# Strided attention on one core: instruction streams moved to a 128-instruction border near their beginning, and constants made by merged operations

## The chip, the cores and the metric

The kernel runs on one core of a Trainium2 chip. A core has five engines with an instruction stream each: TensorE (PE in the profile, with PEld for its weight loads), VectorE (DVE), ScalarE (ACT), GpSimd (POOL) and SyncE (SP), which here only issues transfers. Sixteen DMA engines move the data between HBM and the on-chip memory SBUF. The metric is the time of one execution on the device, in microseconds (us).

## The reference: what is computed

Attention in which every one of the 1024 query positions attends to the same 16 keys, those at the positions 0, 64, 128, ... The inputs Q, K, V are float32 of shape (8, 12, 1024, 64); only the 16 rows of K and V that are attended are ever read.

```python
attend_positions = np.arange(0, seq, stride)          # stride 64: 16 keys
q = Q[:, :, i:i + 1, :]
k = K[:, :, attend_positions, :]
v = V[:, :, attend_positions, :]
scores = np.einsum('bhqd,bhkd->bhqk', q, k) * scale   # scale = 1/sqrt(64)
weights = np.exp(scores - np.max(scores, axis=-1, keepdims=True))
weights = weights / (np.sum(weights, axis=-1, keepdims=True) + 1e-10)
result[:, :, i, :] = np.einsum('bhqk,bhkd->bhqd', weights, v)[:, :, 0, :]
```

## The kernel before

The 96 pairs of batch and head are worked in 24 groups (NG) of four heads (HG). One group is 1 MB of Q and 1 MB of output, so about 50 MB pass through the DMA engines; K and V are 384 KB each.

All transfers are issued by SP, in program order, on one queue. First comes K (`k_raw`, L98), then group 0 of Q (`load(0)`, through the helper `_copy` at L35), then V (`v_raw`, L100), then the Q groups 1 to 9: there are ten buffers for Q (QBUFS) and eight for the output (OBUFS). After that each turn of the main loop issues `store(g)` and then `load(g + 10)`. The first two Q loads are cut into 128 pieces, the later ones into 32.

The head of the kernel builds constants while the first transfers are under way:
- GpSimd makes an identity matrix (`make_identity`, two operations in masks.py), two index tiles (`iota_p`, `col4`, L112 and L114), and by eight copies (L118) the permutation `perm_v`, which spreads the 16 rows of V over 128 partitions; then it clears the larger part of `k_t` (L129).
- VectorE clears the first part of `k_t` (L123) and three weight buffers (L127), works out from the partition number to which of four heads a partition belongs (`slot_i` L132, `slot_f` L137, `s_sel` L139), copies this selector into the last four columns of three value buffers (L145), and makes `mask` from it (L148).
- ScalarE casts K (`key_rows`, L158), VectorE transposes it (`k_r`, L159), and both place it in `k_t` (`keys`, L169).

Then each group goes through the same stations: `cast` to bf16, half by GpSimd (L200) and half by ScalarE (L201); `transpose` on VectorE (L205); `scores`, four matmuls (L212) and the exponential on ScalarE (L223); `values`, the masked V of the group, on GpSimd (L191); `outputs`, eight matmuls (L237) and then reciprocal (L245) and product (L247) on VectorE, with the last part copied by ScalarE (L249) and scaled by GpSimd (L250). Each value buffer carries the selector beside the values, so that the matmul also yields the sum of the weights. The order on each engine is the order of the program (`manual_schedule`); `ahead(g)` puts the casts, transposes and scores of the next groups between the outputs of group g.

Nothing in the program says where an engine's instructions lie in memory. Each engine's stream is fetched in pieces while the kernel runs.

Of the kernel before, what the change touches and what calls it, by code (L numbers as in the profile page):

```python
# [9 lines left out]


FP32 = mybir.dt.float32
BF16 = mybir.dt.bfloat16
I16 = mybir.dt.int16
I32 = mybir.dt.int32
AF = mybir.ActivationFunctionType
ALU = mybir.AluOpType


def _ap_with(ap: bass.AP, new_ap, extra_offset: int = 0) -> bass.AP:  # L20
    return dataclasses.replace(
        ap, ap=[list(p) for p in new_ap], offset=ap.offset + extra_offset
    )


def _copy(nc, out: bass.AP, in_: bass.AP):

    sides = [
        mybir.BassSymbolicTensorAccessPattern(
            ap=side.ap, dtype=side.dtype, bass_ap=side,  # L30
            is_dma=True, for_custom_bir_dma=True,
        )
        for side in (in_, out)
    ]
    return nc.sync.add_instruction(  # L35
        mybir.InstDMACopy(
            name=nc.get_next_instruction_name(), engine=mybir.EngineType.SP,
            ins=sides[:1], outs=sides[1:], queue="qSPDynamicHW",
            mode="Copy",
        )  # L40
    )
# [9 lines left out]
def kernel(  # L51
# [8 lines left out]
    nc = tc.nc  # L60

    B, H, S, D = Q.shape
    NK = S // stride
    scale = 1.0 / math.sqrt(D)

    P = 128
    HG = 4
    NG = B * H // HG
    NC = NG // 2
    SD = S * D  # L70
    KW = P + NK
# [4 lines left out]
    const = ctx.enter_context(tc.tile_pool(name="const", bufs=1))  # L76
# [7 lines left out]

    ctx.enter_context(tc.manual_schedule())


    k_raw = const.tile([P, NC, D], FP32, name="k_raw")
    v_raw = const.tile([P, NC, D], FP32, name="v_raw")
# [3 lines left out]
    def load(g):  # L93
        qn[g] = qn_pool.tile([P, 32 * D], FP32, name="qn", tag="qn")
        n = P if g < 2 else 32
        _copy(nc, qn[g], _ap_with(Q, [[HG * SD // n, n], [1, HG * SD // n]], g * HG * SD))

    nc.sync.dma_start(k_raw, _ap_with(K, kv_src))  # L98
    load(0)
    nc.sync.dma_start(v_raw, _ap_with(V, kv_src))  # L100
    for g in range(1, QBUFS):
        load(g)


    identity = const.tile([P, P], BF16, name="identity")
    make_identity(nc, identity)
    id_v = identity.rearrange("p (c b a k) -> p c b a k", c=2, b=2, a=2)

    perm_v = const.tile([P, 2, 2, 2, 2, NK], BF16, name="perm_v")

    iota_p = const.tile([P, 1], I16, name="iota_p")
    nc.gpsimd.iota(iota_p, pattern=[[0, 1]], base=0, channel_multiplier=1)  # L112
    col4 = const.tile([P, 4], I16, name="col4")
    nc.gpsimd.iota(col4, pattern=[[1, 4]], base=0, channel_multiplier=0)  # L114
    for c in range(2):
        for a in range(2):
            for e in range(2):
                nc.gpsimd.tensor_copy(  # L118
                    out=perm_v[:, c, a, :, e], in_=id_v[:, c, :, a]
                )  # L120

    k_t = const.tile([P, NG, 2, KW], BF16, name="k_t")
    nc.vector.memset(k_t[:, 0:8], 0.0)  # L123
    w_bufs = []
    for i in range(3):
        w = const.tile([P, 8, P], BF16, name=f"w{i}")
        nc.vector.memset(w, 0.0)  # L127
        w_bufs.append(w)
    nc.gpsimd.memset(k_t[:, 8:NG], 0.0)  # L129

    slot_i = const.tile([P, 1], I16, name="slot_i")
    nc.vector.tensor_scalar(  # L132
        out=slot_i, in0=iota_p, scalar1=4, scalar2=3,
        op0=ALU.logical_shift_right, op1=ALU.bitwise_and,
    )
    slot_f = const.tile([P, 1], FP32, name="slot_f")
    nc.vector.tensor_copy(out=slot_f, in_=slot_i)  # L137
    s_sel = const.tile([P, 4], BF16, name="s_sel")
    nc.vector.tensor_scalar(  # L139
        out=s_sel, in0=col4, scalar1=slot_f, scalar2=None, op0=ALU.is_equal  # L140
    )
    v_bufs = []
    for i in range(3):
        v = const.tile([P, 4 * D + 4], BF16, name=f"v{i}")
        nc.vector.tensor_copy(out=v[:, 4 * D :], in_=s_sel)  # L145
        v_bufs.append(v)
    mask = const.tile([P, 4, D], BF16, name="mask")
    nc.vector.tensor_copy(out=mask, in_=s_sel.unsqueeze(2).to_broadcast([P, 4, D]))  # L148

    k_bf = const.tile([P, NC, D], BF16, name="k_bf")  # L150
# [182 lines left out]
```

## Time and profile before

| what | value |
|---|---|
| median of 3 runs | 129.21 us (129.13 to 129.32) |
| span of the profiled execution, first to last instruction | 127.7 us |
| the runs' median beyond this span | 1.5 us |
| PE, DVE, ACT, POOL busy | 50%, 69%, 67%, 63% of the span |
| data moved | 25.95 MB read, 25.17 MB written |
| DMA engines busy with data | 96.7% of the span |
| instruction packets within the span | 5 on queue q14, 2 on queue q8 |

The page gives no other time of the profiled execution than its span. A row of the groups of instructions reads: line, engine, operation, output from input, shapes, count, busy time and the mean of one. A row of the timeline begins with start and duration in us. A row of the table by stages has the stretch, its length, the busy time (and count) of PE, PEld, DVE, ACT and POOL, the granted clock of TensorE, the mean share of the sixteen DMA engines, and GB/s. There a packet is counted whole in the stretch in which it starts, so the share of a short stretch can be above 1. In the rows of queues, the last number is the time of the packets as a share of sixteen engines over the stretch asked for. In the rows of transfers, it is the time from issue to landing.

### The profile page before, as it was taken

How to read it: one execution, taken by the hardware profiler on the slowest of the kernel's cores; microseconds unless marked ns; L12 is line 12 of the kernel's file. 1: busy time of each engine (PE TensorE's matmuls, PEld its weight loads, DVE VectorE, ACT ScalarE, POOL GpSimd, SP SyncE). 2: the span in 40 equal slices, each digit the busy share in tenths (PEclk: the TensorE clock that was granted, in tenths of full speed). 3: DMA queues.
4: the chain of work that ended last, by engine and by line, in shares of the span. 5: the costliest groups of instructions: out<-in, count | busy, mean ns of one | idle time of the engine just before them, and what ended most of it. 6: DMA issues, size and time to landing. Idle time of an engine off the chain costs nothing.

```text
span 127.7 us, 1234 instructions
## 1 busy us (share of the span) xinstructions
PE 63.5 (50%) x292; PEld 29.8 (23%) x292; DVE 88.5 (69%) x167; ACT 86.1 (67%) x120; POOL 80.1 (63%) x89
## 2 busy tenths in 40 slices
PE   0006559256756628653696646366777646410000
PEld 0002223123322313332243313133423313200000
DVE  6956691869698696859769799797987976720000
ACT  4161917886999968999958979979787885320000
POOL 8933709554875876577866997969689694450000
PEclk9999999996799986999559999999856999955555
DMA  2999989998997998989989999999999999999980
GB/s 66 379 320 467 472 349 482 380 452 354 467 482 326 498 413 369 495 362 421 493 357 431 470 380 444 434 403 462 428 393 449 398 428 418 428 426 421 431 352 36
DMA packets 7911, 51.20 MB, mean 401 GB/s; under 512 B 3872, under 2 KB 3872, under 8 KB 3872
## 3 DMA queue, kind: packets, MB, share of 16 engines
q1 hardware_dynamic: 7904, 51.12, 96.7%
q8 instruction: 2, 0.03, 0.1%
q14 instruction: 5, 0.04, 0.1%
HBM read 25.95 MB, written 25.17 MB: 400 GB/s over the span
## 4 chain that ended last, share of the span: by engine, by line
POOL 37%; issue 33%; DVE 10%; PE 6%; ACT 2%; POOLq 1%; DVEq 0%
POOL qb L200 15%; POOL out_sb L250 12%; POOL v L191 10%; PE sc L212 4%; DVE out_sb L247 3%; PE o_ps L237 2%; DVE s_sel L139 2%; POOLq L328 1%; DVE w L127 1%; DVE qt L205 1%; ACT qb L201 1%; DVE rec L245 1%; DVE k_t L123 1%; ACT out_sb L249 1%; ACT k_t L169 0%
## 5 line engine op out<-in xcount | busy, mean ns | idle before, releaser
L237 PE MATMUL o_ps<-v,w 128*128 128x260 bf16 x192 | 37.9, 316 | 37.3 <-DVE out_sb L247 33.2
L250 POOL TENSOR_TENSOR out_sb<-out_sb,rec 128x768 f32<-128x768 f32 x24 | 35.3, 1472 | 29.2 <-ACT out_sb L249 29.2
L247 DVE TENSOR_TENSOR out_sb<-o_ps,rec 128x768 f32<-128x768 f32 (+1 forms) x48 | 39.6, 825 | 1.6
L223 ACT ACTIVATE w<-sc 64x512 bf16<-64x512 f32 x48 | 35.3, 736 | 5.0 <-PE sc L212 4.6
L205 DVE STREAM_TRANSPOSE qt<-qb 128x1024 int32<-128x1024 int32 x24 | 29.5, 1230 | 11.1 <-ACT qb L201 7.1
L212 PE MATMUL sc<-qt,k_t 128*128 128x512 bf16 x96 | 31.7, 463 | 10.4 <-DVE qt L205 10.4
L237 PEld LDWEIGHTS <-w 128*128 128x128 bf16 x192 | 18.6, 108 | 60.5 <-DVE out_sb L247 41.6
L249 ACT COPY out_sb<-o_ps 128x768 f32<-128x768 f32 x24 | 19.2, 800 | 15.8 <-DVE rec L245 15.5
L200 POOL CAST qb<-qn 128x1024 bf16<-128x1024 f32 x24 | 25.0, 1040 | 4.1 <-DMA qn<-in_Q_dram 4.1
L201 ACT CAST qb<-qn 128x1024 bf16<-128x1024 f32 x24 | 25.0, 1047 | 0.7
L245 DVE RECIPROCAL rec<-o_ps 128x12 f32<-128x12 f32 (+1 forms) x72 | 15.1, 210 | 5.6 <-PE o_ps L237 5.2
L191 POOL TENSOR_TENSOR v<-mask,v_rep 128x256 bf16<-128x256 bf16 x24 | 16.1, 670 | 1.0 <-DVE v_rep L184 1.0
L212 PEld LDWEIGHTS <-k_t 128*128 128x128 bf16 x96 | 10.7, 111 | 21.1 <-ACT k_t L169 8.0
L169 ACT COPY k_t<-k_r 32x128 bf16<-32x128 bf16 x20 | 5.9, 296 | 2.3 <-DVE k_r L159 2.0
L129 POOL MEMSET k_t<- 128x4608 bf16 x1 | 3.9, 3937 | 0.0
L184 DVE CAST v_rep<-vp 128x384 bf16<-128x384 f32 x4 | 2.2, 542 | 1.9 <-PE vp L180 1.8
L158 ACT CAST k_bf<-k_raw 128x256 bf16<-128x256 f32 x3 | 1.2, 408 | 2.9 <-DMA k_raw<-in_K_dram 2.9
L139 DVE TENSOR_SCALAR s_sel<-col,slot_f 128x4 bf16<-128x4 int16 x1 | 2.6, 2553 | 0.1
L159 DVE STREAM_TRANSPOSE k_r<-k_bf 128x128 int32<-128x128 int32 x3 | 0.9, 309 | 2.3 <-ACT k_bf L158 2.3
L180 PE MATMUL vp<-v_bf,perm_v 128*128 128x384 bf16 x4 | 1.6, 412 | 1.1 <-DVE v_rep L184 0.6
L158 ACT ACT_TABLE_LOAD x1 | 1.3, 1283 | 0.7 <-PEq L314 0.7
L123 DVE MEMSET k_t<- 128x1152 uint32 x1 | 1.0, 1018 | 1.0 <-PEq L314 1.0
(17 smaller groups left out, 6.6 us busy)
## 6 DMA issues: line engine op xcount, KB each, us to landing
qn<-in_Q_dram SPq DMA_DIRECT2D x24, 1024.0 KB, 16.0
out_dram<-out_sb SPq DMA_DIRECT2D x24, 1024.0 KB, 14.8
k_raw<-in_K_dram SPq DMA_DIRECT2D x1, 384.0 KB, 4.2
v_raw<-in_V_dram SPq DMA_DIRECT2D x1, 384.0 KB, 7.2
```

What stands on the lines that cost most here:

```text
L169: op(k_t[dst : dst + 32, 8 * m + c : 8 * m + 8 : 2, :, col : col + NK], k_r[src : src + 32, 4 * m : 4 * m + 4].rearrange("p n (a k f) -> p ...
L191: nc.gpsimd.tensor_tensor(out=vb[g][:, 0 : 4 * D].rearrange("p (s d) -> p s d", s=4), in0=mask, in1=v_rep[:, g // 2, g % 2].unsqueeze(1).t ...
L200: nc.gpsimd.tensor_copy(out=qb[g][:, 0:half], in_=qn[g][:, 0:half])
L201: nc.scalar.copy(qb[g][:, half:], qn[g][:, half:])
L205: nc.vector.transpose(qt[g].bitcast(I32), qb[g].bitcast(I32))
L212: nc.tensor.matmul(sc, lhsT=k_t[:, g, f, NK * (1 - e) : NK * (1 - e) + P], rhs=_ap_with(q, [q.ap[0], [D, 8], [16 * D, 2], [2, 32]], extra_ ...
L223: nc.scalar.activation(out=_ap_with(wa, [wa.ap[0], [P, 8], [1, 2], [2, 32]], extra_offset=64 * a), in_=sc[64 * a : 64 * a + 64].rearrange( ...
L237: nc.tensor.matmul(ps[:, i, 0 : 4 * D + 4], lhsT=wt[g][:, i0 + i], rhs=vb[g], start=True, stop=True,)
L245: nc.vector.reciprocal(r, ps[:, 0:n, 4 * D : 4 * D + 4])
L247: nc.vector.tensor_tensor(out=to, in0=o, in1=by, op=ALU.mult)
L249: nc.scalar.copy(to, o)
L250: nc.gpsimd.tensor_tensor(out=to, in0=to, in1=by, op=ALU.mult)
```

## The change

Three things change, all in the head.

1. VectorE, GpSimd and SP each get one directive `addr_align(128, max_nops=0)`. The instruction that follows it is placed at the next address that is a multiple of 128 instructions, and the engine gets there by a jump over the padding rather than by running through it. VectorE's and GpSimd's stand before all their work in the kernel's body. SP's stands between the first Q load and V's load.
2. The selector is made from one index tile. `ahead4` holds 64 - 16 s + p for partition p and slot s; its bits 4 and 5 are zero where the partition belongs to the slot. Two operations with a constant operand replace the shift, the cast and the comparison with a per-partition operand. The three weight buffers and the three value buffers become slices of one tile each, so that one clear replaces three and one copy replaces three.
3. `perm_v` is made by four copies of 64 elements per partition, which read each column twice, instead of eight copies of 32.

```diff
+    for engine in (nc.vector, nc.gpsimd):
+        engine.addr_align(128, max_nops=0)
...
     nc.sync.dma_start(k_raw, _ap_with(K, kv_src))
     load(0)
+    nc.sync.addr_align(128, max_nops=0)
     nc.sync.dma_start(v_raw, _ap_with(V, kv_src))
...
-    make_identity(nc, identity)
+    w_all = const.tile([P, 3, 8, P], BF16, name="w_all")
+    v_all = const.tile([P, 3, 4 * D + 4], BF16, name="v_all")
+    w_bufs, v_bufs = [w_all[:, i] for i in range(3)], [v_all[:, i] for i in range(3)]
+
+    nc.gpsimd.iota(ahead4, pattern=[[-16, 4]], base=64, channel_multiplier=1)
+    nc.gpsimd.memset(identity, 0.0)
+    nc.gpsimd.affine_select(
+        out=identity, in_=identity, compare_op=ALU.not_equal, fill=1.0, base=0,
+        pattern=[[-1, P]], channel_multiplier=1,
+    )
...
-    nc.gpsimd.iota(iota_p, pattern=[[0, 1]], base=0, channel_multiplier=1)
-    nc.gpsimd.iota(col4, pattern=[[1, 4]], base=0, channel_multiplier=0)
     for c in range(2):
         for a in range(2):
-            for e in range(2):
-                nc.gpsimd.tensor_copy(
-                    out=perm_v[:, c, a, :, e], in_=id_v[:, c, :, a]
-                )
+            nc.gpsimd.tensor_copy(
+                out=perm_v[:, c, a],
+                in_=id_v[:, c, :, a].unsqueeze(2).to_broadcast([P, 2, 2, NK]),
+            )
     nc.vector.memset(k_t[:, 0:8], 0.0)
-    for i in range(3):
-        w = const.tile([P, 8, P], BF16, name=f"w{i}")
-        nc.vector.memset(w, 0.0)
+    nc.vector.memset(w_all, 0.0)
     nc.gpsimd.memset(k_t[:, 8:NG], 0.0)
-    nc.vector.tensor_scalar(
-        out=slot_i, in0=iota_p, scalar1=4, scalar2=3,
-        op0=ALU.logical_shift_right, op1=ALU.bitwise_and,
-    )
-    nc.vector.tensor_copy(out=slot_f, in_=slot_i)
-    nc.vector.tensor_scalar(
-        out=s_sel, in0=col4, scalar1=slot_f, scalar2=None, op0=ALU.is_equal
-    )
-    for i in range(3):
-        nc.vector.tensor_copy(out=v[:, 4 * D :], in_=s_sel)
+    nc.vector.tensor_single_scalar(out=slot4, in_=ahead4, scalar=48, op=ALU.bitwise_and)
+    nc.vector.tensor_single_scalar(out=s_sel, in_=slot4, scalar=0, op=ALU.is_equal)
+    nc.vector.tensor_copy(out=v_all[:, :, 4 * D :], in_=s_sel.unsqueeze(1).to_broadcast([P, 3, 4]))
     nc.vector.tensor_copy(out=mask, in_=s_sel.unsqueeze(2).to_broadcast([P, 4, D]))
```

More of the change, by code (lines that the diff above doesn't have):

```diff
@@ L7 @@
 from concourse import bass_utils, mybir
-from concourse.masks import make_identity
 from concourse._compat import with_exitstack
@@ L105 @@
     identity = const.tile([P, P], BF16, name="identity")
-    make_identity(nc, identity)
-    id_v = identity.rearrange("p (c b a k) -> p c b a k", c=2, b=2, a=2)
-    perm_v = const.tile([P, 2, 2, 2, 2, NK], BF16, name="perm_v")
-    iota_p = const.tile([P, 1], I16, name="iota_p")
-    nc.gpsimd.iota(iota_p, pattern=[[0, 1]], base=0, channel_multiplier=1)
-    col4 = const.tile([P, 4], I16, name="col4")
-    nc.gpsimd.iota(col4, pattern=[[1, 4]], base=0, channel_multiplier=0)
+    ahead4 = const.tile([P, 4], I16, name="ahead4")
@@ new lines @@
+    slot4 = const.tile([P, 4], I16, name="slot4")
+    s_sel = const.tile([P, 4], BF16, name="s_sel")
+    mask = const.tile([P, 4, D], BF16, name="mask")
+    perm_v = const.tile([P, 2, 2, 2, 2, NK], BF16, name="perm_v")
+    k_t = const.tile([P, NG, 2, KW], BF16, name="k_t")
+    w_all = const.tile([P, 3, 8, P], BF16, name="w_all")
+    v_all = const.tile([P, 3, 4 * D + 4], BF16, name="v_all")
+    w_bufs, v_bufs = [w_all[:, i] for i in range(3)], [v_all[:, i] for i in range(3)]
+    nc.gpsimd.iota(ahead4, pattern=[[-16, 4]], base=64, channel_multiplier=1)
@@ L115 @@
+    nc.gpsimd.memset(identity, 0.0)
[3 more added lines that the diff above has]
+    )
+    id_v = identity.rearrange("p (c b a k) -> p c b a k", c=2, b=2, a=2)
     for c in range(2):
         for a in range(2):
-            for e in range(2):
-                nc.gpsimd.tensor_copy(
-                    out=perm_v[:, c, a, :, e], in_=id_v[:, c, :, a]
-                )
-    k_t = const.tile([P, NG, 2, KW], BF16, name="k_t")
@@ L123 @@
-    nc.vector.memset(k_t[:, 0:8], 0.0)
-    w_bufs = []
-    for i in range(3):
-        w = const.tile([P, 8, P], BF16, name=f"w{i}")
[L127 to L132, printed above, removed]
-        out=slot_i, in0=iota_p, scalar1=4, scalar2=3,
-        op0=ALU.logical_shift_right, op1=ALU.bitwise_and,
-    )
-    slot_f = const.tile([P, 1], FP32, name="slot_f")
-    nc.vector.tensor_copy(out=slot_f, in_=slot_i)
@@ L138 @@
-    s_sel = const.tile([P, 4], BF16, name="s_sel")
-    nc.vector.tensor_scalar(
-        out=s_sel, in0=col4, scalar1=slot_f, scalar2=None, op0=ALU.is_equal
-    )
-    v_bufs = []
-    for i in range(3):
[L144 to L147, printed above, removed]
+            nc.gpsimd.tensor_copy(
+                out=perm_v[:, c, a],
+                in_=id_v[:, c, :, a].unsqueeze(2).to_broadcast([P, 2, 2, NK]),
+            )
```

## The prediction

> **What bounds the kernel now.** I read the page from the bottom up: the transfers first, then who SyncE (SP) waits for, then the tail.
>
> ```profile
> DMA  2999989998997998989989999999999999999980
> HBM read 25.95 MB, written 25.17 MB: 400 GB/s over the span
> q1 hardware_dynamic: 7904, 51.12, 96.7%
> q8 instruction: 2, 0.03, 0.1%
> q14 instruction: 5, 0.04, 0.1%
> qn<-in_Q_dram SPq DMA_DIRECT2D x24, 1024.0 KB, 16.0
> out_dram<-out_sb SPq DMA_DIRECT2D x24, 1024.0 KB, 14.8
> SPq L328 <- DMA out_dram<-out_sb: 11.2, 2, 9.8
> ```
>
> The sixteen DMA engines work for 96.7% of the span on the data queue; the only slack is the first 3 us and the last slice. A 1 MB transfer takes 1.05/400 GB/s = 2.6 us, yet lands 15 to 16 us after its issue: each stands behind some five others in one queue. At the end SP waits 9.8 us for stores that it has long issued. So the kernel is bound by its transfers, and the engines' chain of waits, which the page leads through GpSimd, isn't what sets the end.
>
> The timeline says how early the issues are:
>
> ```profile
> 0.73 0.44 SPq L98 DMA_DIRECT2D k_raw<-in_K_dram  x1
> 1.23 0.73 SPq L35 DMA_DIRECT2D qn<-in_Q_dram  x1
> 2.00 0.59 SPq L100 DMA_DIRECT2D v_raw<-in_V_dram  x1
> 2.63 9.56 SPq L35 DMA_DIRECT2D qn<-in_Q_dram  x9
> 20.91 0.63 SPq L35 DMA_DIRECT2D out_dram<-out_sb  x1
> ```
>
> Twelve transfers, 11.3 MB, are asked for by 12.2 us; at 400 GB/s they last until about 30 us. The first store is issued at 20.91, so the whole head of computation could come about 9 us later before the DMA engines ran dry. Later stores keep at least the margin that a landing time of 14.8 us shows. What remains is the tail. In the table by stages, the DMA share of short stretches at the end:
>
> ```profile
> 123.50:124.00 0.50, 0.00 (x0) 0.00 (x0) 0.00 (x0) 0.00 (x0) 0.00 (x0) 0.50 0.55 229
> 125.35:125.88 0.53, 0.00 (x0) 0.00 (x0) 0.00 (x0) 0.00 (x0) 0.00 (x0) 0.50 0.11 46
> 125.88:126.44 0.56, 0.00 (x0) 0.00 (x0) 0.00 (x0) 0.00 (x0) 0.00 (x0) 0.50 0.04 15
> ```
>
> Each engine has the same data to move, but they don't finish together: half are done by about 124, after 125.35 two are left (0.11 x 16 x 0.53 us = 0.93 us of packets, three of 0.31 us), after 125.88 a single one (0.04 x 16 x 0.56 = 0.36 us, one packet). The last store counts as landed when the last engine is done, at 126.44. So some 2.4 us of the span belong to engines that are late.
>
> Why are they late? The queues q8 and q14 bring instructions, and they do it on the same sixteen engines, in the middle of the saturated stretch. The transfer view finds an instruction packet in the stretches 39 to 40, 98 to 100 and 106 to 107.5 us:
>
> ```profile
> q14 instruction: 1, 0.01, 1.9%
> q14 instruction: 1, 0.01, 1.0%
> q14 instruction: 1, 0.01, 1.3%
> ```
>
> 1.9% of 16 engines for 1 us is 0.30 us. And the data packet behind it is slowed. A stretch of 10 ns holds one packet's start, so share x 16 x 0.01 us is that packet's duration:
>
> ```profile
> 26.10:26.11 0.01, 0.01 (x2) 0.01 (x1) 0.00 (x0) 0.01 (x1) 0.00 (x0) 1.00 7.75 3277
> 39.83:39.84 0.01, 0.01 (x2) 0.01 (x1) 0.00 (x0) 0.01 (x1) 0.00 (x0) 1.00 11.74 3277
> 44.18:44.19 0.01, 0.01 (x1) 0.01 (x1) 0.00 (x0) 0.01 (x1) 0.01 (x1) 1.00 11.82 3277
> 99.29:99.30 0.01, 0.01 (x2) 0.00 (x0) 0.01 (x1) 0.00 (x0) 0.00 (x0) 1.00 10.25 3277
> 110.00:110.01 0.01, 0.01 (x3) 0.01 (x1) 0.00 (x0) 0.01 (x1) 0.00 (x0) 1.00 1.94 819
> 106.93:106.94 0.01, 0.01 (x1) 0.00 (x0) 0.00 (x0) 0.01 (x1) 0.00 (x0) 1.00 4.58 819
> 47.01:47.02 0.01, 0.00 (x0) 0.00 (x1) 0.01 (x1) 0.00 (x0) 0.01 (x1) 0.50 8.69 2458
> ```
>
> A load packet normally takes 7.75 x 0.16 = 1.24 us; the one right behind the fetch at 39.5 takes 1.88 (+0.64), the one behind that at 99.0 takes 1.64 (+0.40). A store packet takes 0.31; behind the fetch at 106.6 it takes 0.73 (+0.42). So an 8 KB fetch holds its engine for 0.30 + 0.64 = 0.94, 0.70 and 0.72 us. The row at 47.01 holds TensorE's 16 KB fetch and a store packet: 1.39 - 0.31 = 1.08 us. At 44.18 a load packet takes 1.89 with no fetch before it; its cause is open.
>
> No view names the engine of a packet. But a packet starts within 10 ns of the end of the one ahead on its engine, and followed so from store to store, the engine that ends last has the fetches at 39.5 and 106.6 and the slow packet at 44.18 (0.94 + 0.65 + 0.72 = 2.3 of its 2.4 us), the second to last the one at 99.0. That is my inference; no view prints it.
>
> **Whose fetches they are.** Fetches of 8 KB are 128 instructions. Busy instructions of each engine between the first and the last of them, and from the start:
>
> ```profile
> 0.00:39.50 39.50, 18.37 (x70) 7.91 (x71) 28.19 (x54) 25.32 (x39) 24.33 (x36) 0.96 0.98 390
> 39.50:106.60 67.10, 41.86 (x206) 20.51 (x205) 55.94 (x104) 57.01 (x77) 51.41 (x50) 0.87 1.00 422
> 0.00:75.00 75.00, 40.35 (x173) 18.45 (x173) 56.57 (x106) 56.87 (x84) 50.65 (x62) 0.91 0.99 403
> PE 63.5 (50%) x292; PEld 29.8 (23%) x292; DVE 88.5 (69%) x167; ACT 86.1 (67%) x120; POOL 80.1 (63%) x89
> ```
>
> Columns are PE, PEld, DVE, ACT, POOL. With the uncounted semaphore instructions (1234 in all, 960 of them counted, so about a quarter more) VectorE's 104 make some 130: it alone passes two borders 128 apart, at 39.5 and 106.6. ScalarE, GpSimd and SP pass one each; the latest, at 99.0, fits SP, which issues only 50 transfers with about as many semaphore waits.
>
> **The change part by part.** *Jumps of VectorE and GpSimd ahead of their work.* Each crosses its border at about 1 us; the code fetch that follows falls before or just at the first data packets and costs the saturated stretch nothing. The next border comes 128 instructions on. VectorE: about 104 counted instructions later, which is near 75 us (x106), or a little later for the five that the change takes out; it still makes one fetch in the stretch, not two. GpSimd has some 84 counted left: none, or one at its very end. The price of a jump itself isn't in the trace: at least 0, since no engine waits for anything unnamed at the borders it passes now; at most the 4.2 us of the row quoted with the third jump, if the code has to come first. Either is covered by the 9 us ahead of the first store; without that cover it would delay every store.
>
> *SP's jump, between the first Q load and V's load.* Behind it stand V's load and nine Q loads. The rows that say what it may cost:
>
> ```profile
> k_raw<-in_K_dram SPq DMA_DIRECT2D x1, 384.0 KB, 4.2
> qn<-in_Q_dram SPq DMA_DIRECT2D x1, 1024.0 KB, 6.3
> 1.00:2.00 1.00, 0.00 (x0) 0.00 (x0) 0.95 (x1) 1.00 (x1) 0.99 (x7) 1.00 0.05 13
> ```
>
> K and the first Q load keep the engines until at most 1.23 + 6.3 = 7.5 us, and at least until 1.8 + 1.44 MB/400 GB/s = 5.4. A transfer's first packet comes about 1.1 us after its issue (0.73 to 1.8). So V may be issued 2.3 to 4.4 us later than 2.00 before a gap opens; I take the middle, 3.4. The stall lies between 0 and 6.3 us (the code queued like that Q load); I take the low end, under 0.5, because the engines that cross borders now never stop there. Cost 0; its gain is the fetch at 99.0 (0.70 us off the second-latest engine), against an early one that meets only small packets.
>
> *Masks and permutation.* The rows of the head:
>
> ```profile
> 1.41 1.26 POOL L118 COPY perm_v<-identity 128x32 bf16<-128x32 bf16 x8
> 2.61 3.94 POOL L129 MEMSET k_t<- 128x4608 bf16 x1
> 2.12 1.56 DVE L127 MEMSET w<- 128x512 uint32 x3
> 3.60 0.10 DVE L132 TENSOR_SCALAR slot_i<-iota_p 128x1 int16<-128x1 int16 x1
> 4.01 2.55 DVE L139 TENSOR_SCALAR s_sel<-col,slot_f 128x4 bf16<-128x4 int16 x1
> 6.60 0.31 DVE L145 COPY v<-s_sel 128x4 bf16<-128x4 bf16 x3
> 7.02 0.30 DVE L159 STREAM_TRANSPOSE k_r<-k_bf 128x128 int32<-128x128 int32 x1
> ```
>
> VectorE loses the cast of the slot, two memset starts (about 0.05 each) and two small copies (0.1 each): 0.4 us. GpSimd's eight copies of 0.16 become four of twice the size, 0.6 to 1.3 us in all, and one iota of 0.13 goes. The s_sel comparison takes 2.55 us where its neighbour of the same kind takes 0.10, and ends at 6.56, with GpSimd's memset (6.55). The new comparison may run in 0.1 or be held up again until that memset's end, some 0.3 us earlier than now. So k_r starts 0.3 to some 1.6 us sooner; next late would be K, which lands at 0.73 + 4.2 = 4.9 us and has to be cast first. All of it lies in front of a store with 9 us of cover: worth 0.
>
> [...]
>
> **The sum.** Profiled execution: span 127.7 us; the runs' median of 129.21 is 1.5 more, which I carry over unchanged. Latest engine: loses 0.72 (fetch at 106.6) and swaps 39.5's 0.94 for one of 0.7 to 0.9 near 75: ends at about 125.6 (124.9 if the slow packet of 44.18 goes too). Second: 125.88 - 0.70 = 125.2. Third, just before 125.35, stays. The end moves from 126.44 to 125.35-125.7, a gain of 0.75 to 1.1; I take 0.9: 129.21 - 0.9 = **128.3**.
>
> **The rivals.**
> *A fetch that stays.* If the one at 99.0 isn't SP's but ScalarE's or GpSimd's, the second engine still ends at 125.88: gain 0.56, 128.65. For it: the view names no owner; against: ScalarE's and GpSimd's counts put theirs earlier.
> *The jumps don't move the end.* The fetches only change places, VectorE's and GpSimd's remaining ones meet the late engine again, or my following of packets is wrong: 129.2. For it: seven fetches in 127 us of transfers are 0.2% of the engines' time.
> [...]
> *SP stalls at its jump.* The code isn't there, and its fetch lies behind the first Q load. Beyond 3.4 us each microsecond is lost whole; with the gain of 0.9 it turns slower from 4.3 us on, and at 6.3 us it gives 129.21 + 2.9 - 0.9 = 131.2. Against it: no border now stops an engine; for it: none of them is passed by a jump.
> [...]
>
> **How the numbers follow.** Forecast 0.48 (its own range 128.0 to 128.6); a fetch that stays 0.15; end not moved 0.20; SP's stall 0.17. About 0.2% (0.26 us) is what a measurement tells from none. Faster: 0.48 + 0.15 = 0.63; same 0.20; slower 0.17. The range takes in the first three, 127.9 to 129.4, and leaves the stall out.
>
> **What the profile after would show.** Right: instruction packets before 3 us, one near 75 to 80, none near 99 or 106; the last engine alone ending near 125.5; V's load issued below 5 us with no dip in the DMA share before 10 us. Wrong: an idle stretch of the DMA engines near 6 to 9 us; fetches that still stand behind 100 us; a tail as long as now; or a first packet later than 1.8 us, since whatever shifts the start of the transfers shifts the end.

## The result, and the profile after

The changed kernel takes 129.00 us in the median of 22 runs (128.70 to 129.39), the kernel before 129.39 (129.07 to 129.73, also 22). The ratio is 0.997, with a 95% interval of 0.9962 to 0.9978: faster by 0.39 us. Forecast were 0.9 us and 128.3, so the direction is right, the size isn't, and, as the experiments show, the reason isn't either: the direction came out right by luck. Each experiment below is compared with runs of the kernel before on the same chip, 129.40 to 129.42 us in the median.

The page of the changed kernel, with the queues and the first transfers from its timeline:

```profile
span 127.2 us, 1226 instructions
HBM read 25.95 MB, written 25.17 MB: 402 GB/s over the span
q1 hardware_dynamic: 7904, 51.12, 96.5%
q8 instruction: 2, 0.03, 0.1%
q14 instruction: 5, 0.04, 0.1%
0.73 0.43 SPq L100 DMA_DIRECT2D k_raw<-in_K_dram  x1
1.23 0.72 SPq L34 DMA_DIRECT2D qn<-in_Q_dram  x1
2.47 0.39 SPq L103 DMA_DIRECT2D v_raw<-in_V_dram  x1
```

The kernel is as much bound by its transfers as before: data take 96.5% of the engines' time, 96.7% before. SP's jump shows in the issue of V: 2.47 instead of 2.00, a price of 0.47 us, and nothing runs dry: by the table by stages no microsecond from 3 to 12 us has a DMA share under 0.97 (before: 0.94). The instruction packets went roughly where the prediction put them: the transfer view of the stretch from 1.5 to 10 us holds three, but the last of them not before 3 us: it stands in the stretch from 6.6 to 6.7. The one from 80 to 83 us holds VectorE's, and none is left between 97 and 127. In this order:

```profile
q14 instruction: 3, 0.02, 0.9%
q14 instruction: 1, 0.01, 19.3%
q14 instruction: 1, 0.01, 0.6%
```

The tail, from the table by stages of the changed kernel (DMA share in the last but one column):

```profile
124.50:125.00 0.50, 0.00 (x0) 0.00 (x0) 0.00 (x0) 0.00 (x0) 0.00 (x0) 0.50 0.16 66
125.00:125.48 0.48, 0.00 (x0) 0.00 (x0) 0.00 (x0) 0.00 (x0) 0.00 (x0) 0.50 0.04 17
125.48:126.00 0.52, 0.00 (x0) 0.00 (x0) 0.00 (x0) 0.00 (x0) 0.00 (x0) 0.50 0.00 0
```

The last data packet ends by 125.48, against 126.44 before: 0.96 us earlier, which looks just like the forecast. But the span is shorter by 0.5 us only. The rest of it went between the last packet and the end of the program: 127.7 - 126.44 = 1.3 us before, 127.2 - 125.48 = 1.7 us now. SP's waits, first of the kernel before, then of the changed one, show where. Both rows belong to the closing barrier; the last number is the longest single wait.

```profile
SPq L328 <- PEq L328: 0.6, 2, 0.4
```
```profile
SPq L319 <- PEq L319: 1.0, 2, 0.8
```

Two questions follow. Is the earlier end of the transfers the work of the jumps? And who is late by 0.4 us in the barrier? Theory F of the expectations is the prediction's gain (fewer fetches, a shorter tail) and a loss that it hadn't priced: 0.4 us because GpSimd's next border comes exactly when no work covers it. Theory M says that the merged operations make the gain, theory R that it is chance in the rate of the Q loads.

### The profile page after: what moved, and what is told of

It is laid out like the page before. It is cut to its first block, busy times and chain, and to the rows that moved or that the text cites. A ratio compares the mean times of both kernels' runs of the same rounds, so it can differ in the third digit from the quotient of the medians.

```text
span 127.2 us, 1226 instructions
## 1 busy us (share of the span) xinstructions
PE 64.3 (51%) x292; PEld 30.2 (24%) x292; DVE 88.4 (69%) x162; ACT 86.0 (68%) x120; POOL 79.5 (62%) x84
## 3 DMA queue, kind: packets, MB, share of 16 engines
q1 hardware_dynamic: 7904, 51.12, 96.5%
## 4 chain that ended last, share of the span: by engine, by line
POOL 35%; issue 32%; DMA 15%; DVE 4%; PE 2%; ACT 1%; POOLq 1%; SPq 0%; DVEq 0%
POOL qb L191 14%; POOL out_sb L241 12%; POOL v_all L182 9%; DMA out_dram<-out_sb 9%; DMA qn<-in_Q_dram 5%; PE sc L203 1%; POOLq L319 1%; DVE out_sb L238 1%; DVE qt L196 1%; DVE v_rep L175 1%; ACT qb L192 1%; PE vp L171 1%; ACT out_sb L240 1%; DVE rec L236 0%; SPq L100 0%
## 5 line engine op out<-in xcount | busy, mean ns | idle before, releaser
L228 PE MATMUL o_ps<-v_all,w_all 128*128 128x260 bf16 x192 | 38.4, 320 | 37.1 <-DVE out_sb L238 32.8
L214 ACT ACTIVATE w_all<-sc 64x512 bf16<-64x512 f32 x48 | 35.2, 734 | 5.5 <-PE sc L203 4.9
L228 PEld LDWEIGHTS <-w_all 128*128 128x128 bf16 x192 | 18.9, 109 | 60.3 <-DVE out_sb L238 41.2
L182 POOL TENSOR_TENSOR v_all<-mask,v_rep 128x256 bf16<-128x256 bf16 x24 | 16.0, 668 | 0.6 <-DVE v_rep L175 0.6
L136 DVE TENSOR_SCALAR slot<-ahead 128x4 int16<-128x4 int16 x1 | 2.5, 2482 | 0.0
```

The lines of the kernel that those rows point to most:

```text
L182: nc.gpsimd.tensor_tensor(out=vb[g][:, 0 : 4 * D].rearrange("p (s d) -> p s d", s=4), in0=mask, in1=v_rep[:, g // 2, g % 2].unsqueeze(1).t ...
L214: nc.scalar.activation(out=_ap_with(wa, [wa.ap[0], [P, 8], [1, 2], [2, 32]], extra_offset=64 * a), in_=sc[64 * a : 64 * a + 64].rearrange( ...
L228: nc.tensor.matmul(ps[:, i, 0 : 4 * D + 4], lhsT=wt[g][:, i0 + i], rhs=vb[g], start=True, stop=True,)
```

## The experiments

The ratio is that of a kernel to the kernel before.

**1. The jumps taken apart from the merged operations.** `no_jumps` is the changed kernel without its three directives; `jumps_only` is the kernel before with them.

```diff
-    for engine in (nc.vector, nc.gpsimd):
-        engine.addr_align(128, max_nops=0)
...
-    nc.sync.addr_align(128, max_nops=0)
```

> The merged operations alone, no jump. F: the fetches stand where they stood before (about 39 and 105 us for VectorE, 57 and 99 for the others), the last DMA engine ends some 2.4 us behind the middle one, and the time is that of before, 129.3 to 129.4. M: 129.0, the whole gain. R: anywhere from 129.0 to 129.4, with the Q loads' packets at 1.22 us in the faster ones.

> The three jumps alone, with the masks and the permutation of before. GpSimd then has about five instructions more behind its jump, so its second border falls ahead of the wait for the last store instead of behind it. F: no pause in the closing barrier, 128.6 to 128.7 where before is 129.4, faster than the whole change. M: 129.4. R: 129.0 to 129.4.

Measured: `no_jumps` 128.58 us, ratio 0.9937 (0.9918 to 0.9957); `jumps_only` 129.48 us, ratio 1.0008 (0.9997 to 1.0018). F's gain falls: the jumps alone bring nothing, though `jumps_only` has no pause in the closing barrier either (longest wait 0.4 us, as before). All the gain, twice that of the whole change, lies with the merged operations; M has the place right and, with 129.0 for `no_jumps`, the size too small. In `no_jumps` the fetches stand late again (44, 62, 98 and 110 us), and yet no kernel of this study is faster than it by more than the noise.

**2. GpSimd's jump left out or moved.** The other two jumps stay in both.

```diff
-    for engine in (nc.vector, nc.gpsimd):
-        engine.addr_align(128, max_nops=0)
+    nc.vector.addr_align(128, max_nops=0)
```

> The changed kernel without GpSimd's jump; VectorE's and SP's stay. Theory F (the gain is the instruction fetches that no longer hit late DMA engines; 0.35 to 0.4 us of it is given back because GpSimd's next border, 128 instructions on, falls into the closing barrier): GpSimd's fetch is back in mid-stream on an engine that isn't the last, the pause between GpSimd's last drain and the semaphore behind it falls from 0.40 to about 0.05 us, and the time is 0.3 to 0.4 us below the changed kernel, near 128.65 where before is 129.4. Theory M (the merged operations make the gain, the jumps nothing): as the changed kernel, 129.0. Theory R (the gain is chance in the rate of the Q loads, 1.22 against 1.24 us per packet): 129.0 to 129.4.

```diff
+    nc.vector.addr_align(128, max_nops=0)
+    nc.gpsimd.addr_align(128, offset=16, max_nops=0)
```

> The changed kernel with GpSimd's jump to 16 instructions behind a border, so that its next border comes 112 instructions on, before the last output product, while the stores still run. F: no pause in the closing barrier; GpSimd's second fetch now falls at about 95 to 105 us, on an engine that is not the last: 128.6 to 128.7 where before is 129.4. M: 129.0. R: 129.0 to 129.4.

Measured: `no_gpsimd_jump` 128.57 us, ratio 0.9942 (0.9923 to 0.996); `gpsimd_border_earlier` 128.72 us, ratio 0.9949 (0.9933 to 0.9965). So GpSimd's jump costs some 0.4 us, most of which goes when its second border is passed earlier. `no_gpsimd_jump` equals `no_jumps` within 0.01 us: the jumps of VectorE and SP neither cost nor gain. Both times lie near those that F names for these runs, but with experiment 1 they speak for its loss at GpSimd's border alone, not for its gain.

The tails agree. The stretch in which the last packets start, in the kernel before, in `jumps_only`, and in `before_aligned` (the kernel before without any jump, its buffers moved as in experiment 3):

```profile
125.50:126.00 0.50, 0.00 (x0) 0.00 (x0) 0.00 (x0) 0.00 (x0) 0.00 (x0) 0.50 0.12 49
```
```profile
125.50:126.00 0.50, 0.00 (x0) 0.00 (x0) 0.00 (x0) 0.00 (x0) 0.00 (x0) 0.50 0.12 49
```
```profile
125.50:126.00 0.50, 0.00 (x0) 0.00 (x0) 0.00 (x0) 0.00 (x0) 0.00 (x0) 0.50 0.00 0
```

The jumps alone leave the tail nearly as long as it was; it ends earlier where the buffers are moved, jumps or not.

Why the moved fetches gain nothing is argued, not shown. From about 4 us on the DMA engines are busy almost without a break (the data packets that start from 4 to 124 us take 100.5% of that stretch, each counted whole where it starts); two stretches of the changed kernel:

```profile
2.00:2.50 0.50, 0.00 (x0) 0.00 (x0) 0.50 (x1) 0.01 (x1) 0.50 (x4) 1.00 0.26 65
4.00:4.50 0.50, 0.00 (x0) 0.00 (x0) 0.50 (x2) 0.00 (x0) 0.50 (x1) 1.00 0.99 361
```

What an engine loses after that, to the fetch at 6.6 us for one, it should carry to its last store. Experiment 6 shows that this can't be the whole reason.

**3. What of the merged operations makes the gain.** In `no_jumps` the head comes only 0.3 us earlier (the transpose of K at 6.70 instead of 7.02), far inside the cover ahead of the first store, so I looked for something else that it changes. It drops several tiny tiles and joins others, and so all later buffers move. By the allocation of the two programs the ten Q buffers begin at 53,376 + 8192 n bytes of each partition before, and at 53,248 + 8192 n after; the output buffers follow. 53,376 is 128 bytes behind a multiple of 512 (and of 256), 53,248 is a multiple. This is theory A; theory O says that it is the operations after all. `before_aligned` changes no instruction of the kernel before:

```diff
+    const.tile([P, 192], BF16, name="pad")
     k_bf = const.tile([P, NC, D], BF16, name="k_bf")
```

> The kernel before with one unused tile of 384 bytes per partition ahead of the later tiles, so that every Q and output buffer starts at a multiple of 512 bytes in its partition instead of 128 bytes behind one; not one instruction is changed. Theory A (the merged operations helped only because fewer small tiles moved the buffers to such a border; a load packet then takes 1.22 instead of 1.24 us while loads run alone): load packets of 1218 ns from the start, time 128.6 to 128.9 where before is 129.4. Theory O (the operations themselves made the gain, through an earlier or shorter head): 129.4, load packets of 1240 ns.

`merged_shifted` does the reverse to `no_jumps`, with `const.tile([P, 64], BF16, name="pad")` at the same place:

> The merged operations without jumps, with an unused tile of 128 bytes that puts the Q and output buffers back to 128 bytes behind a border of 512. A: the gain is gone, 129.2 to 129.4, load packets of 1240 ns before 31 us. O: 128.6 as without the tile.

Measured: `before_aligned` 128.74 us, ratio 0.9953 (0.9935 to 0.9971); `merged_shifted` 129.48 us, ratio 1.0004 (0.9987 to 1.0021). An unused tile gives the gain to the old kernel, and another takes it from the new one. So theory O falls, and theory R with it: the rate of the loads follows the place of the buffers. The load packets agree. Stretches of 10 ns that hold the start of one 32 KB load packet (share x 0.16 us is its duration), while loads run alone: `before_aligned`, the whole change, `merged_shifted`:

```profile
26.09:26.10 0.01, 0.01 (x2) 0.01 (x1) 0.01 (x1) 0.00 (x0) 0.00 (x0) 0.50 7.61 3277
```
```profile
26.10:26.11 0.01, 0.01 (x1) 0.00 (x0) 0.00 (x0) 0.00 (x0) 0.00 (x0) 0.50 7.62 3277
```
```profile
26.79:26.80 0.01, 0.01 (x1) 0.00 (x0) 0.00 (x0) 0.01 (x1) 0.01 (x1) 0.50 7.79 3277
```

These are 1.22, 1.22 and 1.25 us; the prediction's row of the kernel before at 26.10 has 1.24. Once stores run between the loads, the difference is gone, here in the kernel before and in `merged_shifted`:

```profile
33.53:33.54 0.01, 0.00 (x0) 0.00 (x0) 0.01 (x1) 0.01 (x1) 0.01 (x1) 1.00 7.61 3277
```
```profile
34.21:34.22 0.01, 0.01 (x2) 0.01 (x1) 0.00 (x0) 0.01 (x1) 0.01 (x1) 1.00 7.62 3277
```

Eight loads of two such packets on each engine run alone: 16 x 0.02 to 0.03 us, 0.3 to 0.5 us. The time of all data packets of an engine, the share of the q1 row times the span, falls by more: 96.7% of 127.7 = 123.5 us before, 96.7% of 126.9 = 122.7 in `before_aligned`. The shares are rounded: summed over the packet records behind the views it is 123.48 and 122.81, a difference of 0.67, and the measured gain is 0.66 us there. Of the 0.67, 0.42 lie in the 32 KB load packets, 0.12 in the packets of 8 KB (stores and the first two Q loads) and 0.12 in the 256-byte packets of K and V; why the last of these differ, no run here shows.

**4. Which buffers, and which border.** `loads_shifted` has `no_jumps` with only the Q buffers 128 bytes off; `stores_shifted` with only the output buffers off; `merged_shifted256` with all of them 256 bytes behind a border of 512. The edit of `loads_shifted`, beside the jumps (`stores_shifted` has no `pad` and a `gap` of 64 elements, `merged_shifted256` a `pad` of 128 and no `gap`):

```diff
+    gap_pool = ctx.enter_context(tc.tile_pool(name="gap", bufs=1))
     out_pool = ctx.enter_context(tc.tile_pool(name="outsb", bufs=OBUFS))
...
+    const.tile([P, 64], BF16, name="pad")
+    gap_pool.tile([P, 192], BF16, name="gap")
```

> As the last one, but the output buffers are brought back to the border by a second unused tile of 384 bytes; only the Q buffers stand 128 bytes off. A, if it is the loads' packets that cost: 129.1 to 129.4. A, if stores cost as well (their packets take 311 ns in all runs so far, so I do not expect it): between 128.7 and 129.1. O: 128.6.

> The merged operations without jumps; Q buffers at the border of 512 bytes, output buffers 128 bytes behind one. If only the loads' buffers matter: 128.6 where before is 129.4, store packets of 311 ns as ever. If the stores' buffers matter too: 128.8 or more.

> The merged operations without jumps and with all Q and output buffers 256 bytes behind a border of 512. If the border that counts is one of 256 bytes: 128.6, load packets of 1218 ns from the start. If it is one of 512 bytes: 129.4, packets of 1240 ns.

Measured: `loads_shifted` 129.41 us, ratio 0.9997 (0.9977 to 1.0017); `stores_shifted` 128.60 us, ratio 0.9942 (0.9925 to 0.9959); `merged_shifted256` 128.67 us, ratio 0.9933 (0.9912 to 0.9953). It is the buffers that loads write into, and a multiple of 256 bytes is enough. The load packet's row in each, in this order:

```profile
26.05:26.06 0.01, 0.01 (x1) 0.00 (x0) 0.00 (x0) 0.01 (x1) 0.00 (x0) 0.50 7.75 3277
```
```profile
26.41:26.42 0.01, 0.01 (x2) 0.00 (x0) 0.00 (x0) 0.01 (x1) 0.00 (x0) 0.50 7.62 3277
```
```profile
26.46:26.47 0.01, 0.01 (x1) 0.00 (x0) 0.00 (x0) 0.01 (x1) 0.00 (x0) 0.50 7.62 3277
```

Off the border the packet takes 1.7% longer (7.75 against 7.62); why, no run here shows. Output buffers 128 bytes off, which the stores read, go free (128.60 us); the loss is in the buffers that loads write, and in mixed traffic it is gone (7.61 and 7.62 in the two rows between stores above).

**5. GpSimd's jump by itself.** Both start from `no_jumps`:

```diff
+    nc.gpsimd.addr_align(128, max_nops=0)
```

> The merged operations with GpSimd's jump alone, buffers at the border. If the whole loss of the jumps is GpSimd's border in the closing barrier (0.35 us between its last drain and the semaphore behind it): 128.95 to 129.0, as the whole change. If the jumps of VectorE and SP cost their share: 128.7 to 128.8.

```diff
+    nc.gpsimd.addr_align(128, offset=16, max_nops=0)
```

> The merged operations, buffers at the border, and GpSimd's jump alone, to 16 instructions behind its border, so that its next one is passed while stores still run. If the loss of GpSimd's jump is its border in the closing barrier: 128.6, and 0.05 us between its last drain and the semaphore behind it, instead of 128.9. If the jump itself or its early fetch costs: 128.9.

Measured: `gpsimd_jump_only` 128.93 us, ratio 0.9971 (0.9953 to 0.9988), as slow as the whole change; `gpsimd_jump_earlier_alone` 128.74 us, ratio 0.9949 (0.9933 to 0.9965). SP's row of the closing barrier, in this order:

```profile
SPq L317 <- PEq L317: 0.9, 2, 0.8
```
```profile
SPq L317 <- PEq L317: 0.6, 2, 0.4
```

The pause comes and goes with the place of the border, not with the jump. The rows name TensorE's queue (PEq), but in the records behind the views SP goes on after a step of GpSimd: the semaphore instruction behind GpSimd's last drain starts 0.39 to 0.40 us after it in the whole change, in `gpsimd_jump_only` and in `after_shifted`, and 0.04 after it in all others. What GpSimd does in the pause stays open; its second instruction packet comes only behind it, in the stretch from 127.6 to 127.7 of the whole change. The time gives back 0.2 of the 0.35 us, half-way between the two expectations; the remaining 0.15 against `no_jumps` lies within the spread of single runs, and may as well be a price of the jump.

**6. The sum.** `after_shifted` is the whole change with the 128 bytes of `merged_shifted`.

> The whole change with an unused tile of 128 bytes that takes the buffers off the border again. If the change is the sum of a gain by the border (0.8) and a loss by GpSimd's jump (0.4): slower than before, 129.75 to 129.9 where before is 129.4. If the jumps bring something of their own once the loads are slow: 129.4 or less.

Measured: 129.76 us, ratio 1.0033 (1.0019 to 1.0048). Without the border of the buffers the same change is slower than the kernel before, by 0.35 us, as much as GpSimd's pause. And its data ends no earlier to speak of, at 126.35 us by the packet records, though two fewer fetches of 8 KB meet the busy engines. Transfer views from 4 to 126.4 us, first of the kernel before, then of `after_shifted`:

```profile
q14 instruction: 5, 0.04, 0.1%
```
```profile
q14 instruction: 3, 0.02, 0.0%
```

So in this execution even fetches that are gone from the stretch didn't shorten the tail. What makes the last engines late stays open.

## Why the prediction was wrong

- *What bounds the kernel*: right. Everything that moved the time moved the transfers or what follows the last of them.
- *Whose fetches they are, and where they go*: right in the main. The 128 instructions to a fetch of 8 KB roughly fit the records: VectorE has 133 instructions between its two fetches before, and 135 from its jump to the one fetch it has left in the stretch. VectorE's two became one at 81.7 us, somewhat later than said, SP's at 99 and GpSimd's at 57 went to the head, GpSimd's second came at its very end.
- *The price of SP's jump*: right, 0.47 us against "under 0.5". The rival of a long stall fell.
- *"The code fetch that follows falls before or just at the first data packets and costs the saturated stretch nothing"*: this step failed, and with it the step that put the lateness of the last engine (2.3 of its 2.4 us) down to its fetches and one slow packet. The term of 0.9 us for the jumps measured 0: `jumps_only` differs from before by +0.06, `no_gpsimd_jump` from `no_jumps` by -0.01. A fetch came as late as 6.6 us, when the engines hardly had a gap any more; but `after_shifted`, with two fetches fewer behind 4 us, ends its data only 0.09 us earlier, so more than the place of the fetches was wrong, and the rest of the reason stays open. The 10 ns by which I followed packets from one to the next don't hold throughout: by the records of the kernel before, half of the 8 KB packets that start from 75 to 110 us do so within 7 ns of the latest end of any packet, but a quarter 28 ns or more behind it. The tail that ended 0.96 us earlier in one execution seemed to confirm the prediction; most of that was the faster loads, since `before_aligned` ends 0.77 us earlier without a jump (125.67 by the packet records).
- *"GpSimd has some 84 counted left: none, or one at its very end"*: I saw the place and gave it no price. I took it that an engine that passes a border never stops, from a kernel in which GpSimd's only wait without a named releaser is one of 0.2 us ahead of its first operation. Between two steps of the closing barrier it measured 0.35 to 0.4 us.
- *"Masks and permutation ... worth 0"*: the operations are worth 0. The first comparison, `slot`, now is the one held up until GpSimd's clear ends:

```profile
2.67 3.94 POOL L134 MEMSET k_t<- 128x4608 bf16 x1
4.15 2.48 DVE L136 TENSOR_SCALAR slot<-ahead 128x4 int16<-128x4 int16 x1
7.15 0.30 DVE L150 STREAM_TRANSPOSE k_r<-k_bf 128x128 int32<-128x128 int32 x1
21.14 0.63 SPq L34 DMA_DIRECT2D out_dram<-out_sb  x1
```

  The transpose of K starts at 7.15 instead of 7.02 and the first store is issued at 21.14 instead of 20.91, where 0.3 to 1.6 us sooner was forecast: without the jumps it does start 0.3 sooner (6.70 in `no_jumps`), and GpSimd's jump, behind which its first operation of the kernel's body starts at 1.27 instead of 0.73, gave that back. The cover of 9 us made all of it free, as predicted. What I left out is that the tiles of the head stand in front of the big buffers in memory: this term should have been -0.7 to -0.8 us.
- The two wrong terms and the missing one add to the result: -0.8 for the buffers, 0 for the fetches, +0.4 for GpSimd's border, -0.4.

The rival that the jumps don't move the end was the right one about the jumps. `jumps_only` shows it (1.0008); GpSimd's 0.4 us in the closing barrier is the exception.

The version that beats both is the merged operations without jumps, 128.58 us, 0.9937 of the kernel before.

## What to carry to other kernels

Before a diff that adds, drops or merges tiles is priced by its operations, look where the buffers land that follow them: here 128 bytes of offset in the buffers that loads write were worth 0.7 to 0.8 us, more than anything the changed instructions did. Try big buffers that transfers write at a multiple of 256 bytes: here that was as fast (128.67 us) as a multiple of 512 (128.58), and tiles allocated behind the Q buffers didn't shift them (`stores_shifted`, 7.62). And before a gain is written to late fetches, test it by itself: here moving them to an earlier time gained nothing (1.0008).

## What the runs showed of the hardware that I had not expected

- A load packet of 32 KB took 1.22 us into rows at a 256-byte border and 1.24 to 1.25 us into rows 128 bytes behind one, as long as loads alone were in flight; between stores it took 1.22 us either way. Why the stores hide it stays open.
- In the kernel before, GpSimd's fetch came at 57.5 us, in the middle of its work, and the view of its waits shows none there without a named releaser; the border between two steps of the closing barrier went with a pause longer by 0.35 us. A jump cost about 0.5 us: the next operation came 0.47 us later on SP (V's issue, 2.47 for 2.00), 0.54 on GpSimd (1.27 for 0.73) and 0.57 on VectorE (1.61 for 1.04). This kernel hides those of VectorE and SP: with and without them it takes the same time within 0.01 us.
- The sixteen engines ended unevenly with five fetches of 8 KB behind 4 us and with three: by the packet records the last one ends 2.4 us after half of them are done in the kernel before, and 2.2 in `after_shifted`.
